# A two-layer trunk: a ring of six adaLN buffers in the first stage, projection weights two tiles ahead, one PE order through the early part, one modulation vector fewer on PE

## The chip, the cores and the metric

The kernel runs on one core of a Trainium2 chip. Its engines have a queue each and run side by side: PE (TensorE, matmuls and transposes), DVE (VectorE), ACT (ScalarE), POOL (GpSimd) and SP (SyncE, which issues most DMAs here). The metric is the device time of one execution in microseconds. Nearly all of the work of the program before the first MLP stands in the first 502 of 2436 us, and the change is made there.

## The reference

x is 256 × 2048, f32, one sequence. Layer 0 mixes tokens with a conformer convolution, layer 1 with differential attention; both are followed by a squared-ReLU MLP of hidden size 8192. The sizes: D = 2048, and each modulation vector needs a 2048 × 2048 matrix (16 MB) against the condition.

```python
cond = jax.nn.silu(c)
for i in range(DEPTH):
    mod = cond @ ada_w[i] + ada_b[i]
    sh_m, sc_m, g_m, sh_f, sc_f, g_f = [m[:, None, :] for m in jnp.split(mod, 6, axis=-1)]
    h = x * (1.0 + sc_m) + sh_m
    y = conformer_conv(h, ...)  # layer 0; layer 1: diff_attention
    x = layer_norm(DEEPNORM_ALPHA * x + g_m * y, ln_mix_g[i], ln_mix_b[i])
    h = x * (1.0 + sc_f) + sh_f
    y = squared_relu_mlp(h, mlp_w1[i], mlp_b1[i], mlp_w2[i], mlp_b2[i])
    x = layer_norm(DEEPNORM_ALPHA * x + g_f * y, ln_ffn_g[i], ln_ffn_b[i])

def conformer_conv(h, w1, b1, w_dw, b_dw, g, b, w2, b2):
    u = h @ w1 + b1                                  # pw1, 2048 x 4096
    a, gt = jnp.split(u, 2, axis=-1)
    u = a * jax.nn.sigmoid(gt)                       # GLU
    u = lax.conv_general_dilated(...) + b_dw         # causal, depthwise, width 31
    u = jax.nn.silu(layer_norm(u, g, b))             # over channels
    return u @ w2 + b2                               # pw2, 2048 x 2048
```

## The kernel before

**Products.** A f32 product is made of three matmuls. ACT rounds a weight half (128 × 1024) to its high part (L462, in later stages L515), DVE, or in places POOL, subtracts to get the low part (L463, L516), and PE multiplies high × high, low × high and high × low (L476 to L478, L551 to L554). The activations are split in the same way (L393, L396). One "half" of a weight tile is twelve such matmuls. A weight tile is 1 MB.

**adaLN vectors.** A vector is summed up in one of two ways, and always from 1 MB tiles that SP loads (L215). A *DVE step* multiplies one tile's two row blocks by the condition and adds them to `aacc` (L243 for the first block, L245 for the others, 128 × 1024 each); at the end PE sums over partitions (`apt`, L228) and DVE adds the bias. A *PE step* multiplies the tile by the condition (`aps`, L286, eight matmuls, spread over column groups), ACT copies the result (`arow`, L290), PE transposes it (`apt`, L269).

**First stage.** pw1 has eight groups of 512 columns. Groups 2, 3 (`ROT`) and 0, 1 (`RES`) are worked first, in five slices of the contraction (`SLICES`: 2, 4, 4, 4 and 2 chunks of 128 rows), since only the slice of the modulated input has to be ready. While slice s is multiplied, the tiles of scale (by DVE) and shift (by PE) for slice s + 1 are used, by `ada_pair` at the halves in `pair_at`; then `end_ada` (PE `apt`, transposes of x, modulation, split by ACT and DVE) makes the next slice's input. `ada_raw` says where an adaLN tile lies: of every four, two are in the `araw` pool and two in halves of `conv_ux`, a buffer that the convolution uses later. Projection weights run four tiles ahead: `load_w` is called four times before the stage and then whenever `split_half` has used up a tile. In the first and last slice a weight tile is half a megabyte (2 chunks of 512 columns).

**T1.** Groups 4 to 7 follow, 32 halves. Between them a written plan (`at(n, ...)`) puts the convolution of the groups that are ready: `glu`, `conv_shift` (copies by ACT and DVE that shift rows), `conv_taps`, `conv_products`, `conv_out`, `conv_tok`, `conv_stats`. `other_vectors` (transposes of four small parameter vectors into columns, L845 to L851) is one item of it, at n = 2. `ADA_T1` DVE steps (20) are spread evenly over the 32 halves, from `dve_q`, which holds the gate G_M and the first half of the scale SC_F.

**Transition.** Between T1 and pw2 stands the last group's chain, `glu(7)`, `conv_shift(7)`, `conv_products`, `conv_out`, `conv_tok`, `conv_stats`, then the channel LayerNorm (L635), then `swish` (PE transposes L1109, ACT silu), three times ahead of pw2. The calls `fill(n)` put n PE steps (SH_F, then the second half of SC_F, from `pe_q`) between these, by `FILL`. Their loads run three ahead, in two `araw` buffers and half of `conv_ux`.

**T2.** pw2 has 32 halves in four groups of 512 columns (`out_proj`). After a half `pump_t2` runs, sixteen times with effect, and spreads what is left of `dve_q` and `pe_q` evenly.

**What sets the order.** `manual_schedule` keeps an engine's instructions in the order in which they are written. Before, the first part (up to and with `conv_shift(7)`) is written so for PE, DVE, ACT and SP together, and a second one for PE alone opens behind it; where none is open, a scheduler sets the order. DVE's is opened again at the start of pw2.

Of the kernel before, what the change touches and what calls it, by code (L numbers as in the profile page):

```python
# [78 lines left out]
def trunk(  # L79
# [371 lines left out]
    def load_raw(src, name):  # L451
        raw = wraw.tile([P, 2048], F32, tag="raw", name=f"w_{name}")[:, :src.shape[1] * NG]
        rv = raw.rearrange("p (a h n) -> p a h n", a=src.shape[1], h=src.shape[2])
        for h in range(src.shape[2]):
            raws["dma"] = nc.sync.dma_start(rv[:, :, h, :], src[:, :, h, :])
        return raw

    def split_raw(rq, name):
# [3 lines left out]
        nc.scalar.copy(hi, rq)  # L462
        nc.vector.tensor_tensor(lo, rq, hi.bitcast(F32), op=ALU.subtract)  # L463
# [381 lines left out]
    def other_vectors():  # L845
        adab.append(as_cols(small_rows["adab1"], "adab1"))
        lnc = as_cols(small_rows["ln"], "ln")
        b1c = as_cols(small_rows["b1"], "b1")
        subg = as_cols(small_rows["subg"], "subg")
        nc.vector.tensor_scalar(subg, subg, 1.0 - LAMBDA_INIT, None, ALU.mult)  # L850
        cv.update(lnc=lnc, b1c=b1c, subg=subg)  # L851
# [726 lines left out]
```

## Time and profile before

| | |
|---|---|
| median of 3 runs | 2439.43 us (2437.01 to 7178.41) |
| profiled execution | 2438.22 us |
| its span, mean granted clock | 2436.4 us, 0.977 |
| first stage | 0 to 196.9 us |
| T1, its start included | 196.9 to 357.8 us |
| transition | 357.8 to 410.9 us |
| T2 | 410.9 to 502.0 us |
| all that follows | 502.0 to 2436.4 us |

The starts are those of the first pw1 matmul after a slice's `end_ada` (slices 2 to 5 start at 70.6, 109.3, 148.0 and 176.8 us), of the last matmul of the first stage, of the end of pw1 and of the first matmul of pw2's bias (L550). Times are microseconds. A row of the stretches gives, for each engine, its busy time in the stretch and the number of instructions; PEclk is the TensorE clock granted there, DMA share is how busy the 16 DMA engines were. A row of waits gives the engine and line that waited, what it waited for, the total, the number of times and the longest. A row of grouped lines gives busy time, mean ns, then idle time ahead of it. MATMUL rows of the timeline are pipelined, so they overlap.

### The profile page before, as it was taken

To read this page: it belongs to the slowest core of one execution; us is meant where nothing else is said; L and a number is where in the kernel's file an instruction comes from. 1 tells how busy PE (TensorE), PEld (TensorE's weight loads), DVE (VectorE), ACT (ScalarE), POOL (GpSimd) and SP (SyncE) were. 2 spreads that over 40 slices of the span, in tenths; PEclk is the share of its full clock that TensorE was granted. 3 is DMA by queue.
4 is the path that set the end of the run, shared out by engine and by line. 5 is a ranking of instruction groups with operands and counts; after the bars stand their busy time and mean duration, and the time that the engine had idled before them with its cause. 6 is when DMAs were issued, how large, how long until landed. Compare 5 with 4: busy or idle time off the path is not lost.

```text
span 2436.4 us, 28627 instructions
## 1 busy us (share of the span) xinstructions
PE 2294.2 (94%) x11223; PEld 1816.7 (75%) x11223; DVE 1744.6 (72%) x1973; ACT 1070.2 (44%) x1376; POOL 243.6 (10%) x162
## 2 busy tenths in 40 slices
PE   3888997989989999999998999998999999999997
PEld 2566763767878888888876888886788888888886
DVE  4666873569798888878868777886867555555566
ACT  2335754344434434434434544443443443443442
POOL 0000000122150000000014200012204000000002
PEclk8999998999999999999999999998999999999999
DMA  9977678857988887888875676685686555555563
GB/s 337 323 245 245 230 260 293 310 202 273 344 294 317 304 308 284 311 314 299 295 255 187 207 238 223 232 289 191 221 287 223 185 186 192 190 188 195 185 224 104
DMA packets 278252, 608.55 MB, mean 250 GB/s; under 512 B 11166, under 2 KB 52708, under 8 KB 264804
## 3 DMA queue, kind: packets, MB, share of 16 engines
q1 hardware_dynamic: 277876, 606.41, 72.1%
q8 instruction: 88, 1.44, 0.2%
q10 hardware_dynamic: 240, 0.30, 0.1%
q14 instruction: 48, 0.39, 0.0%
HBM read 604.54 MB, written 2.13 MB: 249 GB/s over the span
## 4 chain that ended last, share of the span: by engine, by line
PE 81%; DVE 8%; DMA 5%; ACT 2%; issue 2%; SPq 1%; POOL 1%; DVEq 0%; ACTq 0%; POOLq 0%
PE w_ps L551 18%; PE w_ps L553 18%; PE w_ps L554 18%; DMA aw<-in_ada_w_dram 2%; PE cv L755 2%; PE pw_ps L476 2%; PE pw_ps L477 2%; PE pw_ps L478 2%; DMA conv_ux<-in_ada_w_dram 2%; PE aps L286 1%; DVE wl_w L516 1%; PE pw_ps L551 1%; PE qkv_q_ps L554 1%; PE qkv_q_ps L553 1%; PE qkv_q_ps L551 1%
## 5 line engine op out<-in xcount | busy, mean ns | idle before, releaser
L516 DVE TENSOR_TENSOR wl_w<-w_w,wh_w 128x1024 fp32r<-128x1024 f32 x502 | 633.6, 1280 | 333.1 <-ACT wh_w L515 332.7
L515 ACT CAST wh_w<-w_w 128x1024 fp32r<-128x1024 f32 x512 | 537.7, 1053 | 754.2 <-PE w_ps L554 589.1
L551 PE MATMUL w_ps<-wh_w,hm_hi 128*128 128x512 f32 x1024 | 403.8, 394 | 4.8 <-ACT hm_hi L393 4.8
L553 PE MATMUL w_ps<-wl_w,u_hi 128*128 128x512 f32 x1024 | 399.2, 390 | 6.5 <-DVE wl_w L516 6.4
L553 PE MATMUL w_ps<-wl_w,hm_hi 128*128 128x512 f32 x1024 | 400.8, 391 | 4.7 <-DVE wl_w L516 4.6
L554 PE MATMUL w_ps<-wh_w,hm_lo 128*128 128x512 f32 x1024 | 400.9, 392 | 0.9 <-DVE hm_lo L396 0.9
L551 PE MATMUL w_ps<-wh_w,u_hi 128*128 128x512 f32 x1024 | 400.0, 391 | 0.0
L554 PE MATMUL w_ps<-wh_w,u_lo 128*128 128x512 f32 x1024 | 398.6, 389 | 0.0
L312 DVE SCALAR_TENSOR_TENSOR acc<-adaw,cond,acc 128x2048 f32<-128x2048 f32 (+1 forms) x105 | 244.1, 2325 | 0.1
L551 PEld LDWEIGHTS w_ps<-wh_w,hm_hi 128*128 128x128 f32 x1024 | 193.4, 189 | 49.0 <-ACT hm_hi L393 6.5
L553 PEld LDWEIGHTS w_ps<-wl_w,u_hi 128*128 128x128 f32 x1024 | 192.2, 188 | 48.5 <-DVE wl_w L516 9.3
L553 PEld LDWEIGHTS w_ps<-wl_w,hm_hi 128*128 128x128 f32 x1024 | 193.3, 189 | 45.1 <-DVE wl_w L516 5.9
L554 PEld LDWEIGHTS w_ps<-wh_w,hm_lo 128*128 128x128 f32 x1024 | 193.3, 189 | 43.1 <-DVE hm_lo L396 2.5
L551 PEld LDWEIGHTS w_ps<-wh_w,u_hi 128*128 128x128 f32 x1024 | 192.2, 188 | 42.1 <-issue 2.5
L554 PEld LDWEIGHTS w_ps<-wh_w,u_lo 128*128 128x128 f32 x1024 | 192.2, 188 | 40.0
L516 POOL TENSOR_TENSOR wl_w<-w_w,wh_w 128x1024 fp32r<-128x1024 f32 x10 | 24.0, 2405 | 1096.6 <-ACT wh_w L515 1096.6
L476 PE MATMUL pw_ps<-wh_pw,h_hi 128*128 128x512 f32 x256 | 108.9, 425 | 8.6 <-ACT h_hi L393 8.4
L463 DVE TENSOR_TENSOR wl_pw<-w_pw,wh_pw 128x1024 fp32r<-128x1024 f32 x64 | 77.9, 1224 | 46.2 <-ACT wh_pw L462 45.5
L477 PE MATMUL pw_ps<-wl_pw,h_hi 128*128 128x512 f32 x256 | 103.8, 405 | 0.5 <-DVE wl_pw L463 0.5
L478 PE MATMUL pw_ps<-wh_pw,h_lo 128*128 128x512 f32 x256 | 103.3, 403 | 0.0
L245 DVE SCALAR_TENSOR_TENSOR aacc<-aw,cond,aacc 128x1024 f32<-128x1024 f32 (+2 forms) x80 | 81.0, 1012 | 30.8 <-DMA aw<-in_ada_w_dram 29.1
L462 ACT CAST wh_pw<-w_pw 128x1024 fp32r<-128x1024 f32 x64 | 66.2, 1049 | 33.2 <-PE pw_ps L478 13.0
(338 smaller groups left out, 3214.5 us busy)
## 6 DMA issues: line engine op xcount, KB each, us to landing
w_w<-in_mlp_w_dram SPq DMA_DIRECT2D x256, 1024.0 KB, 5.3
adaw<-in_ada_w_dram SPq DMA_DIRECT2D x96, 1024.0 KB, 5.4
aw<-in_ada_w_dram SPq DMA_DIRECT2D x60, 1024.0 KB, 6.8
w_pw<-in_conv_pw_w_dram SPq DMA_DIRECT2D x56, 512.0 KB, 5.3
...
```

What stands on the lines that cost most here:

```text
L245: nc.vector.scalar_tensor_tensor(st["acc"], wv[:, kc % per, :], cond[:, kc:kc + 1], st["acc"], ALU.mult, ALU.add)
L312: nc.vector.scalar_tensor_tensor(st["acc"], w, cond[:, kc:kc + 1], st["acc"], ALU.mult, ALU.add)
L462: nc.scalar.copy(hi, rq)
L463: nc.vector.tensor_tensor(lo, rq, hi.bitcast(F32), op=ALU.subtract)
L476: nc.tensor.matmul(pss[t], lhsT=xh, rhs=wh, start=(kc == first), stop=False)
L477: nc.tensor.matmul(pss[t], lhsT=xh, rhs=wl, start=False, stop=False)
L478: nc.tensor.matmul(pss[t], lhsT=xl, rhs=wh, start=False, stop=(kc == last))
L515: nc.scalar.copy(hi, rq)
L516: eng.tensor_tensor(lo, rq, hi.bitcast(F32), op=ALU.subtract)
L551: nc.tensor.matmul(pss[tt], lhsT=xh, rhs=wh, start=(kc == 0 and job["bias"] is None), stop=False)
L553: nc.tensor.matmul(pss[tt], lhsT=xh, rhs=wl, start=False, stop=False)
L554: nc.tensor.matmul(pss[tt], lhsT=xl, rhs=wh, start=False, stop=(kc == nk - 1))
```

## The change

It has six parts.

1. *Ring of six.* In the first stage `ada_raw` goes round six places: two of `conv_ux`, two in the projection weights' `raw` pool, two of `araw`.
2. *Projection weights two ahead.* Two `load_w` and two more adaLN tiles stand ahead of the stage; in return the slices of two chunks load full 1 MB tiles that hold two groups, so their order becomes 2, 3, 0, 1. At T1's start two more `load_w` bring the weights back to four ahead.
3. *Places in the stage.* `pair_at` and the half at which `end_ada` stands are moved.
4. *Four places for `other_vectors`.* One vector each at n = 2, 3, 6 and 7.
5. *One PE order.* PE's `manual_schedule` opens at the very start and goes through to T2. The load of the silu table is moved ahead of the end of the first part. `conv_shift(7)` has 6 copies on ACT and 10 on DVE in place of 8 and 8.
6. *One vector fewer on PE.* The second half of SC_F goes from `pe_q` (24 steps, now 16) to `dve_q` (24, now 32). `ADA_T1` is 24 in place of 20, and the fills of the transition are 2, 1, 1, 2 (and the one ahead of the gate), with one call fewer.

```diff
-ADA_T1 = 20
-FILL = (3,1,3,2,1)
+ADA_T1 = 24
+FILL = (2, 1, 1, 2)
...
-SHIFT_END = ("act", "dve", "act", "dve")
+END_ACT = (0, 3, 6, 9, 12, 15)
...
             n_raw[0] += 1
-            if n_raw[0] % 4 in (3, 0):
-                return ux[:, n_raw[0] % 4 // 3 * 2048:(n_raw[0] % 4 // 3 + 1) * 2048]
+            n = n_raw[0] % 6
+            if n in (2, 3):
+                return ux[:, (n - 2) * 2048:(n - 1) * 2048]
+            if n in (4, 5):
+                return wraw.tile([P, 2048], F32, tag="raw", name=name)
         return araw.tile([P, 2048], F32, tag="araw", name=name)
...
     add_dve(SC_F, 0, m_scf)
+    add_dve(SC_F, 8, m_scf)
     pe_loads = []
-    for v, m, f00 in ((SH_F, m_shf, 0), (SC_F, m_scf, 8)):
-        for f0 in range(f00, KC, 4):
-            loads, steps = ada_slice_steps(0, v, f0, 4, m, apart=True)
...
+    for f0 in range(0, KC, 4):
+        loads, steps = ada_slice_steps(0, SH_F, f0, 4, m_shf, apart=True)
...
-                if (SHIFT_END if j == 7 else SHIFT)[(r - b) % 4] == "act":
+                if (4 * b + r in END_ACT) if j == 7 else SHIFT[(r - b) % 4] == "act":
...
-    def other_vectors():
-        adab.append(as_cols(small_rows["adab1"], "adab1"))
-        lnc = as_cols(small_rows["ln"], "ln")
...
+    def other_vectors(n):
+        if n == 0:
+            adab.append(as_cols(small_rows["adab1"], "adab1"))
+        elif n == 1:
+            cv.update(lnc=as_cols(small_rows["ln"], "ln"))
...
     engines = mybir.EngineType
-    first_part = tc.manual_schedule(engines={engines.PE, engines.DVE, engines.Activation, engines.SP})
+    early_pe = tc.manual_schedule(engines={engines.PE})
+    early_pe.__enter__()
+    first_part = tc.manual_schedule(engines={engines.DVE, engines.Activation, engines.SP})
...
-    order = [tuple(g for gs in zip(ROT, RES) for g in gs)] * len(SLICES)
+    order = [ROT + RES if nf == 2 else tuple(g for gs in zip(ROT, RES) for g in gs) for f0, nf in SLICES]
     n_first = len(RES + ROT)
-    w_src = [(f"pw1_{g}_{s}", pw1v[:, f0:f0 + nf, :, g * 256:(g + 1) * 256])
-             for s, (f0, nf) in enumerate(SLICES) for g in order[s]]
+    w_src = [(f"pw1_{g}_{s}", pw1v[:, f0:f0 + nf, :, g * 256:(g + 4 // nf) * 256])
+             for s, (f0, nf) in enumerate(SLICES) for g in order[s][::4 // nf]]
...
-    for _ in range(N_RAW):
+    for _ in range(2):
         load_w()
+    for _ in range(2):
+        ada_load.pop(0)()
...
-        pair_at = {4: (0, 1, 2, 3) if n_half == 4 else (0, 2, 4, 5), 2: (2, 5), 0: ()}[nxt]
+        pair_at = {4: (0, 1, 2, 3) if n_half == 4 else (1, 3, 5, 7), 2: (2, 4), 0: ()}[nxt]
...
-                if nxt and h == (3 if n_half == 4 else 6):
+                if nxt and h == (5 if nxt == 2 else n_half - 1):
                     pending()
                     end_ada(s + 1)
...
-            if last and n == 1:
-                pending()
+                if nf == 2:
+                    pending()
+            if last and n == 2:
                 glu(ROT[0])
...
-    at(2, other_vectors)
+    for n in range(4):
+        at((2, 3, 6, 7)[n], other_vectors, n)
...
     for _ in range(2):
+        load_w()
         dve_loads.pop(0)()
...
     glu(7)
     conv_shift(7)
+    warm = small.tile([P, 1], F32, tag="warm", name="warm", bufs=1)
+    nc.scalar.activation(warm, ones[:, 0:1], AF.Silu)
     first_part.__exit__(None, None, None)
-    early_pe = tc.manual_schedule(engines={engines.PE})
-    early_pe.__enter__()
...
     tick(10)
-    fill(FILL[2])
...
-    fill(FILL[3])
+    fill(FILL[2])
...
     for c2 in range(3):
         swish(c2)
-        if c2 < 2:
-            fill(FILL[4])
+    fill(FILL[3])
```

How this moves instructions stands in the order of each queue. First SP's transfers in the first stage, before, from the first adaLN tile of slice 1 (chunk 2) on; `aw` tiles and `conv_ux` are adaLN tiles of 1 MB, `w_pw_2_1` is the projection weight of group 2 and slice 1 (slices are numbered from 0 in names).

```order
L215 DMA aw_1_2_0_205<-in_ada_w_dram 128x4x512
L215 DMA aw_0_2_0_207<-in_ada_w_dram 128x4x512
L215 DMA conv_ux<-in_ada_w_dram 128x4x512 x2
L455 DMA w_pw_2_1_233<-in_conv_pw_w_dram 128x4x256 x2
L455 DMA w_pw_0_1_240<-in_conv_pw_w_dram 128x4x256 x2
L455 DMA w_pw_3_1_269<-in_conv_pw_w_dram 128x4x256 x2
L455 DMA w_pw_1_1_296<-in_conv_pw_w_dram 128x4x256 x2
L215 DMA aw_1_2_2_313<-in_ada_w_dram 128x4x512
L215 DMA aw_0_2_2_315<-in_ada_w_dram 128x4x512
L215 DMA conv_ux<-in_ada_w_dram 128x4x512 x2
```

The same place of SP after:

```order
L218 DMA aw_1_2_0_152<-in_ada_w_dram 128x4x512
L218 DMA aw_0_2_0_154<-in_ada_w_dram 128x4x512
...
L218 DMA aw_1_2_1_205<-in_ada_w_dram 128x4x512
L218 DMA conv_ux<-in_ada_w_dram 128x4x512 x2
L218 DMA aw_0_2_2_227<-in_ada_w_dram 128x4x512
L459 DMA w_pw_2_1_237<-in_conv_pw_w_dram 128x4x256 x2
L218 DMA aw_1_2_3_288<-in_ada_w_dram 128x4x512
L218 DMA aw_0_2_3_290<-in_ada_w_dram 128x4x512
L459 DMA w_pw_0_1_300<-in_conv_pw_w_dram 128x4x256 x2
```

The eight adaLN tiles for the second slice have one projection tile between them instead of four.

Second, PE in the transition, before, from the transposes of the shift vector's first part to the first matmul of pw2; `aps` is an adaLN step, `gb_p` the gate's broadcast, `sw` the swish transposes.

```order
L269 MATMUL apt_3_0_2932<-ident,arow_3_0_2909 128x128 x4
L644 MATMUL gb_p<-ident,mod_2_116 16x128
L286 MATMUL aps_3_4_2925<-conv_ux,condr 32x512 x4
L286 MATMUL aps_3_4_2925<-aw_3_4_2_2911,condr 32x512 x4
L286 MATMUL aps_3_4_2925<-aw_3_4_3_2930,condr 32x512 x4
L286 MATMUL aps_3_8_2981<-conv_ux,condr 32x512 x4
L269 MATMUL apt_3_4_2987<-ident,arow_3_4_2961 128x128 x4
L286 MATMUL aps_3_8_2981<-aw_3_8_1_2955,condr 32x512 x4
L1109 MATMUL sw_3002<-ident,vtok 128x128 x4
L286 MATMUL aps_3_8_2981<-aw_3_8_2_2963,condr 32x512 x4
L1109 MATMUL sw_3018<-ident,vtok 128x128 x4
```

PE at the same place after:

```order
L656 MATMUL gb_p<-ident,mod_2_116 16x128
L272 MATMUL apt_3_0_2951<-ident,arow_3_0_2940 128x128 x4
L289 MATMUL aps_3_4_2974<-aw_3_4_0_2847,condr 32x512 x4
L1127 MATMUL sw_2983<-ident,vtok 128x128 x4
L1127 MATMUL sw_2993<-ident,vtok 128x128 x4
L1127 MATMUL sw_3003<-ident,vtok 128x128 x4
L289 MATMUL aps_3_4_2974<-conv_ux,condr 32x512 x4
L289 MATMUL aps_3_4_2974<-aw_3_4_2_2942,condr 32x512 x4
L289 MATMUL aps_3_4_2974<-aw_3_4_3_2979,condr 32x512 x4
L289 MATMUL aps_3_8_3069<-conv_ux,condr 32x512 x4
L562 MATMUL pw_0_ps_3034<-pw2b_hl,one_2678 128x512 x2
```

One adaLN step stands between the gate's broadcast and the first swish transpose instead of five, and the three swish transposes follow one another. Ahead of this, in the group-7 `glu`, PE's eight transposes (`pa`, `pg`) had two adaLN steps among them before and have none now.

Third, DVE in T2 around the end of pw2's first group, before; `wl_pw` is a subtraction for a half's low part, `aacc` the DVE step, `pw_g` a group's output.

```order
L516 TENSOR_TENSOR wl_pw_1_0_0_3243<-w_pw_1_0_3240,wh_pw_1_0_0_3242 128x1024
L516 TENSOR_TENSOR wl_pw_1_0_1_3259<-w_pw_1_0_3240,wh_pw_1_0_1_3258 128x1024
L245 SCALAR_TENSOR_TENSOR aacc_4_0_2485<-aw_4_0_5_3262,cond,aacc_4_0_2485 128x1024 x2
L697 TENSOR_TENSOR pw_g_3304<-pw_0_ps_3055,conv_ux 128x512
...
L516 TENSOR_TENSOR wl_pw_1_1_1_3322<-w_pw_1_1_3286,wh_pw_1_1_1_3321 128x1024
L516 TENSOR_TENSOR wl_pw_1_2_0_3351<-w_pw_1_2_3348,wh_pw_1_2_0_3350 128x1024
L516 TENSOR_TENSOR wl_pw_1_3_0_3390<-w_pw_1_3_3387,wh_pw_1_3_0_3389 128x1024
```

DVE at the same place after:

```order
L528 TENSOR_TENSOR wl_pw_1_0_0_3229<-w_pw_1_0_3226,wh_pw_1_0_0_3228 128x1024
L528 TENSOR_TENSOR wl_pw_1_0_1_3245<-w_pw_1_0_3226,wh_pw_1_0_1_3244 128x1024
L248 SCALAR_TENSOR_TENSOR aacc_4_8_3048<-aw_4_8_2_3248,cond,aacc_4_8_3048 128x1024 x2
L709 TENSOR_TENSOR pw_g_3282<-pw_0_ps_3034,conv_ux 128x512
...
L528 TENSOR_TENSOR wl_pw_1_1_1_3293<-w_pw_1_1_3264,wh_pw_1_1_1_3292 128x1024
L528 TENSOR_TENSOR wl_pw_1_2_0_3321<-w_pw_1_2_3318,wh_pw_1_2_0_3320 128x1024
L248 SCALAR_TENSOR_TENSOR aacc_4_8_3048<-aw_4_8_3_3340,cond,aacc_4_8_3048 128x1024 x2
```

A DVE step comes after every four halves in T2 in place of after every eight.

More of the change, by code (lines that the diff above doesn't have):

```diff
@@ L348, in trunk @@
     add_dve(SC_F, 0, m_scf)
+    add_dve(SC_F, 8, m_scf)
     pe_loads = []
-    for v, m, f00 in ((SH_F, m_shf, 0), (SC_F, m_scf, 8)):
-        for f0 in range(f00, KC, 4):
-            loads, steps = ada_slice_steps(0, v, f0, 4, m, apart=True)
-            pe_loads.extend(loads)
-            pe_q.extend(steps)
+    for f0 in range(0, KC, 4):
+        loads, steps = ada_slice_steps(0, SH_F, f0, 4, m_shf, apart=True)
+        pe_loads.extend(loads)
+        pe_q.extend(steps)
     m_gf = mod_tile(0, G_F)
@@ L451, in load_raw @@
     def load_raw(src, name):
-        raw = wraw.tile([P, 2048], F32, tag="raw", name=f"w_{name}")[:, :src.shape[1] * NG]
-        rv = raw.rearrange("p (a h n) -> p a h n", a=src.shape[1], h=src.shape[2])
-        for h in range(src.shape[2]):
+        raw = wraw.tile([P, 2048], F32, tag="raw", name=f"w_{name}")
+        rv = raw.rearrange("p (a h n) -> p a h n", a=src.shape[1], h=2)
+        for h in range(2):
             raws["dma"] = nc.sync.dma_start(rv[:, :, h, :], src[:, :, h, :])
-        return raw
+        if src.shape[1] == 4:
+            rw = raw.rearrange("p (q a n) -> p q a n", q=2, a=2)
+        else:
+            rw = raw.rearrange("p (a h q n) -> p q a h n", a=2, h=2, q=2)
+        return [rw[:, q] for q in range(2)]
     def split_raw(rq, name):
@@ L461, in split_raw @@
         lo = wsp.tile([P, 1024], F32R, tag="wlo", name=f"wl_{name}")
-        nc.scalar.copy(hi, rq)
-        nc.vector.tensor_tensor(lo, rq, hi.bitcast(F32), op=ALU.subtract)
         hv = hi.rearrange("p (a n) -> p a n", n=NG)
         lv = lo.rearrange("p (a n) -> p a n", n=NG)
-        return [(hv[:, a, :], lv[:, a, :]) for a in range(1024 // NG)]
+        if len(rq.shape) == 4:
+            hq, lq = [v.rearrange("p a (h n) -> p a h n", h=2) for v in (hv, lv)]
+        else:
+            hq, lq = hv, lv
+        nc.scalar.copy(hq, rq)
+        nc.vector.tensor_tensor(lq, rq, hq.bitcast(F32), op=ALU.subtract)
+        return [(hv[:, a, :], lv[:, a, :]) for a in range(2)]
     def mm_parts(pss, pair, parts, kc0, first, last):
@@ L843, in tap_columns @@
         nc.vector.tensor_reduce(eye, ident.rearrange("p (r c) -> p c r", c=32), axis=AX.X, op=ALU.add)
-    def other_vectors():
-        adab.append(as_cols(small_rows["adab1"], "adab1"))
-        lnc = as_cols(small_rows["ln"], "ln")
[L848 to L851, printed above, removed]
+    def other_vectors(n):
[3 more added lines that the diff above has]
+            cv.update(lnc=as_cols(small_rows["ln"], "ln"))
+        elif n == 2:
+            cv.update(b1c=as_cols(small_rows["b1"], "b1"))
+        else:
+            cv.update(subg=as_cols(small_rows["subg"], "subg"))
+            nc.vector.tensor_scalar(cv["subg"], cv["subg"], 1.0 - LAMBDA_INIT, None, ALU.mult)
     engines = mybir.EngineType
-    first_part = tc.manual_schedule(engines={engines.PE, engines.DVE, engines.Activation, engines.SP})
+    early_pe = tc.manual_schedule(engines={engines.PE})
+    early_pe.__enter__()
+    first_part = tc.manual_schedule(engines={engines.DVE, engines.Activation, engines.SP})
     first_part.__enter__()
@@ L1069, in fill @@
             tick()
-    warm = small.tile([P, 1], F32, tag="warm", name="warm", bufs=1)
-    nc.scalar.activation(warm, ones[:, 0:1], AF.Silu)
     fill(FILL[0])
```

7 lines of the change are left out of this document (3 added, 4 removed).

## The prediction

> **What bounds the kernel now.** I read the page first, to see which engine sets the time.
>
> ```profile
> span 2436.4 us, 28627 instructions
> PE 2294.2 (94%) x11223; PEld 1816.7 (75%) x11223; DVE 1744.6 (72%) x1973; ACT 1070.2 (44%) x1376; POOL 243.6 (10%) x162
> PE 81%; DVE 8%; DMA 5%; ACT 2%; issue 2%; SPq 1%; POOL 1%; DVEq 0%; ACTq 0%; POOLq 0%
> ```
>
> PE is busy for 94% of the span, so a gain is a stretch in which PE stands still now, or PE work that goes away. The change touches only what runs before the first MLP. So the second view is busy time by stretch, with cuts at the starts of slices 2 to 5 of the first stage, the start of T1 (pw1 groups 4 to 7), the transition and T2 (pw2), and with ten microseconds of slice 1 apart.
>
> ```profile
> core 0: us, PE busy (x) PEld busy (x) DVE busy (x) ACT busy (x) POOL busy (x), PEclk, DMA share, GB/s
> 0.00:70.60 70.60, 30.75 (x148) 18.21 (x148) 31.74 (x58) 18.92 (x32) 1.98 (x11) 0.88 1.01 342
> 70.60:109.30 38.70, 31.30 (x148) 21.03 (x149) 25.71 (x37) 10.95 (x14) 0.00 (x0) 0.96 0.97 343
> 109.30:148.00 38.70, 32.31 (x150) 22.15 (x149) 25.99 (x38) 11.89 (x15) 0.00 (x0) 0.91 0.95 319
> 148.00:176.80 28.80, 26.44 (x133) 19.78 (x133) 21.16 (x36) 12.09 (x16) 0.00 (x0) 0.94 0.48 151
> 176.80:196.90 20.10, 19.87 (x96) 16.21 (x96) 11.30 (x16) 13.94 (x21) 0.00 (x0) 1.00 0.78 262
> 196.90:207.30 10.40, 0.95 (x5) 0.47 (x3) 9.28 (x16) 9.34 (x13) 0.00 (x0) 0.68 0.76 268
> 207.30:357.80 150.50, 148.75 (x1356) 107.42 (x1356) 117.91 (x169) 94.63 (x145) 0.00 (x0) 0.99 0.68 231
> 357.80:410.90 53.10, 35.89 (x277) 11.66 (x275) 14.53 (x38) 20.21 (x35) 0.72 (x1) 0.81 0.84 306
> 410.90:502.00 91.10, 91.10 (x443) 64.88 (x440) 55.07 (x58) 34.84 (x42) 12.68 (x5) 1.00 0.89 309
> 50.00:60.00 10.00, 0.37 (x4) 0.20 (x8) 2.99 (x4) 0.00 (x0) 0.00 (x0) 0.50 1.06 377
> ```
>
> Three of these are bound in three ways. In slices 1 to 3 the DMA share is 0.95 or more and PE idles: the transfers set the pace. At T1's start (10.4 us, PE 0.95) PE waits for other engines. In the transition (53.1 us, PE 35.9) much of PE's work is adaLN steps put there as filler. T1's body and T2 are full of PE. Third, who ends PE's waits in the first stage, and the longest of them:
>
> ```profile
> PE aps L286 <- DMA aw<-in_ada_w_dram: 24.4, 4, 14.6
> PE aps L286 <- DMA conv_ux<-in_ada_w_dram: 11.3, 3, 4.4
> PE pw_ps L476 <- ACT h_hi L393: 8.4, 2, 6.8
> 59.63 1.94 PE L286 MATMUL aps<-aw,condr 128*32 128x512 f32 x8 [14.57 <-DMA aw<-in_ada_w_dram]
> ```
>
> PE waits 35.7 us for adaLN tiles, 14.57 of them in one piece for slice 2's tiles. The sum below goes against the profiled execution, 2438.22 us (span 2436.4 and 1.8 around it); the median of the runs shown, 2439.43, is 1.2 above it.
>
> **First stage: ring of six, projection weights two ahead.** The total of buffers is unchanged and so are the bytes; what moves is which transfer is issued first. By the order of SP's transfers, slice 2's last adaLN tile is the 17th megabyte issued instead of the 20th, since two projection tiles less stand ahead and one more is put behind. Three tiles of 1.0486 MB at the 377 GB/s of the 50–60 row are 3 × 2.78 = 8.3 us, out of a wait of 14.57: slice 2 starts about 8 us earlier, for sure within 0 and 8.3.
>
> A full slice moves 12 tiles (8 adaLN, 4 projection), 12.58 MB. At 377 GB/s that is 33.4 us; it takes 38.7. PE is busy 31.3 and 32.3 of it, DVE 25.7 and 26.0, so transfers kept in flight would win at most 5.3 per slice, 10.6 in both. I take 8: `end_ada` now stands behind the last half, its chain of apt, transposes and ACT splits is covered by no matmul, and a projection tile two ahead makes DVE's in-order subtraction wait sooner. Slices 4 and 5 (48.9 us, PE 46.3 busy) have nothing to give. Sum −16; ends 0 and −18.9, and with all 2.4 us that PE idles in slices 4 and 5, −21.3.
>
> The Trainium skill ("DMA: Bandwidth & Descriptors", Specifications) gives about 358 GB/s of HBM per core: by it a slice is 35.1 us and the gain 3.6 in place of 5.3. The trace moved 377 for ten microseconds, so the measured rate decides.
>
> **T1's start.** PE's two waits and DVE's in T1:
>
> ```profile
> PE pt_subg L134 <- DVE cols_adab L136: 5.7, 1, 5.7
> PE pt_b L134 <- DVE conv_ux L806: 3.7, 1, 3.7
> L245 DVE SCALAR_TENSOR_TENSOR aacc<-aw,cond,aacc 128x1024 f32<-128x1024 f32 x37 | 47.4, 1282 | 0.7
> L243 DVE TENSOR_SCALAR aacc<-aw,cond 128x1024 f32<-128x1024 f32 x3 | 2.2, 750 | 4.9 <-DMA aw<-in_ada_w_dram 4.9
> L463 DVE TENSOR_TENSOR wl_pw<-w_pw,wh_pw 128x1024 fp32r<-128x1024 f32 x29 | 35.5, 1225 | 18.2 <-ACT wh_pw L462 17.7
> ```
>
> `other_vectors` asks for four transposes at once, and PE's third half stands behind them: 9.4 us. Split over plan points 2, 3, 6 and 7, only one vector's chain stands there. The tile for which DVE waited 4.9 is now issued ahead of a weight tile. Against this, 24 adaLN steps in 32 halves put the third step ahead of the third half (24·3/32 = 2.25, before 20·3/32 = 1.875), 2 × 1.28 = 2.6 us more on DVE there. The lo split that PE needs waits on DVE anyway, so not all 9.4 goes: −5, ends 0 and −9.4.
>
> **T1's body.** Four more DVE steps of two 1.28 us instructions: 10.3 us. DVE is busy 117.9 of 150.5, so 32.6 us are free, and PE fills 148.75: hidden, 0. Without that cover it is +10.3. The silu table load moves within ACT, which has 55.9 us free here: 0.
>
> **Transition.** The timeline's rows in order of time (start, duration, what ran, in brackets the wait ahead of it), and PE's waits for tiles:
>
> ```profile
> 363.11 1.07 PE L286 MATMUL aps<-aw,condr 128*32 128x512 f32 x8 [2.89 <-DMA aw<-in_ada_w_dram]
> 366.82 5.45 ACT L737 COPY conv_x<-u 32x571 f32<-32x571 f32 x8 [0.58 <-DVE u L806]
> 366.82 3.74 DVE L739 COPY conv_x<-u 32x571 f32<-32x571 f32 x8
> 385.30 2.37 DVE L635 TENSOR_SCALAR vtok<-vtok,cln_mv,cln_rs 128x512 f32<-128x512 f32 x5
> 390.68 1.94 PE L286 MATMUL aps<-aw,condr 128*32 128x512 f32 x8 [2.86 <-DMA aw<-in_ada_w_dram]
> 398.27 0.79 PE L1109 MATMUL sw<-ident,vtok 128*128 128x128 f32 x4
> 410.88 0.71 PE L550 MATMUL pw_ps<-pw2b_hl,one 4*128 4x512 f32 x2
> PE aps L286 <- DMA aw<-in_ada_w_dram: 12.6, 6, 2.9
> ```
>
> Step by step. (1) With one PE order, all eight pa/pg transposes of glu(7) stand ahead of the tile that made PE wait 2.89 and work 1.07 in between: −3.9. (2) `conv_shift(7)` was 8 copies on ACT, 5.45, and 8 on DVE, 3.74; with 6 and 10 it ends with DVE's 10 × 0.467 = 4.7: −0.8. (3) The first swish transpose stood at 398.27, behind five adaLN steps that follow the gate's broadcast (L644), though its input is normalised by 385.3 + 2.4 = 387.7; of these one is left, and I take all but its wait out of the 10.6 us: −10. (4) From the first sw to pw2 it is 12.6 us, four adaLN steps strung between the later sw and their waits; the four now stand in a row behind three sw, 3 × 0.8 + 4 × 1.94 = 10.2 at the slow clock: −2. That is −16.7. A cross-check: 14 tiles stand ahead of pw2 before and 9 after; 53.1/14 = 3.8 a tile, 5 × 3.8 = 19. Between the two I take −18. Ends: −10, if the tiles that are left wait each for its transfer (12.6 in 6 now), and −20.
>
> The Trainium skill ("TensorE: Matmul & The Clock Gate", Part 1) has PE's clock fall to half after an idle window of some 3.4 us, and rise again after as much work, which speaks against taking filler out: by it pw2 would start at half clock, an estimate of +1.7. The trace agrees that this happens: the same eight matmuls take 1.07 at 363 and 1.94 at 390.68, and the clock was 0.50 in the 50–60 row.
>
> **T2.** What is taken from the transition comes back here in part: 8 DVE steps instead of 4, 7 PE steps instead of 10.
>
> ```profile
> DVE aacc L245 <- DMA aw<-in_ada_w_dram: 19.1, 4, 6.0
> DMA to landing us min/median/max: 5.0/6.7/6.8
> ```
>
> PE saves 3 × 1.07 = 3.2 of 91.1. DVE has 55.1 busy and 19.1 waited, 4.8 a step, since each tile is asked for right before its step. Four more steps are 10.3 of work. In the order three of the eight have their tile issued a step earlier, so five wait: 24. Together 55.1 + 10.3 + 24 = 89.4, against PE's 88: no slack is left, and the subtraction that PE's next half needs stands behind each wait. I take 3.2 saved and 8 lost: +5, ends −3 (all hidden) and +13 (10.3 + 24 − 19.1 − 3.2 = 12).
>
> **Sum:** −16 − 5 + 0 − 18 + 5 = −34: 2438.2 − 34 = 2404. After pw2 nothing is changed.
>
> **Rivals.**
> A. All covers hold. The stage gives 21.3, T1's start 9.4, the transition 20, T2 3.2: −54, 2384. For it: the stage is plainly transfer-bound (share 0.95 to 1.01). Against: every chain would have to be free.
> B. The ring isn't six buffers. Two of them are shared with the projection weights and rotate with them, so a projection tile waits until an adaLN tile is consumed, and DVE, which consumes both, waits for the projection tile two ahead: one wait replaces another and the stage gives nothing. Then −5 − 18 + 5 = −18: 2420, with T2 at its worse end 2428. For it: the bytes are the same and DVE waits there as well. Against: slice 2's last tile is issued three megabytes earlier whatever happens.
> C. T2 bound by DVE: +13 there, 2412. For it: the sum of 89.4. Against: POOL takes a few of its subtractions.
> D. Slower: T1 bound by DVE. If each of its 24 steps waited 4.8 as T2's do, 115 us would stand against 22.3 left free: +93, 2497. It makes the kernel slower at all from (22.3 + 34)/24 = 2.3 us a step. Against: 37 instructions of L245 in T1 with 0.7 us idle ahead of them.
>
> **How the numbers follow.** Forecast 0.53 (own range 2392 to 2414), A 0.18, B 0.17, C 0.08, D 0.04. The range takes A's end and B's with T2's worse end, and leaves out D and what lies beyond A: 2384 to 2430. Two per cent, about what a measurement here can tell from no change, is 48.8 us: 2390.6 and 2488.2. A and a sliver of the forecast lie below: faster 0.2. Only D lies above: slower 0.04. Within 0.76.
>
> **What would show it.** Slice 2 starting at about 62 us (was 70.6) and slices 2 and 3 at 35 each confirm the stage; 38 each is B. T1's start: the stretch with PE idle 5 in place of 10. Transition: pw2's first matmul 35 us after T1's last one in place of 53. T2: 96 in place of 91, with waits at the adaLN step on DVE of 24 or more; under 91 it is A, over 100 C. The forecast is wrong if the MLP after it changes, or if T1's body grows by more than 3.

## The result and the profile after

The changed kernel takes 2446.56 us (median of 10 runs), the kernel before 2442.09 in the same sessions: a ratio of 1.0025 with a 95% interval of 1.0014 to 1.0035. It is a quarter of a per cent slower; forecast was 2404. One run of the kernel before took 7178.41 us; no other did, and the median does not show it. The profiled execution took 2448.23 us, its span 2446.4 against 2436.4.

The busy time by stretch for the changed kernel, cut at the same events: starts of slices 2 to 4 (64.41, 103.96, 140.71), the end of the first stage (190.78), the third half of T1 (195.2), the end of T1, the first matmul of pw2 and the starts of pw2's groups. A slice starts with the first product of its own here. In the kernel before, one half of the old slice still stands behind `end_ada` ahead of slices 3 and 4: the starts given for it (109.3 and 148.0) are those behind this half, while the first products after `end_ada` come at 106.45 and 145.20. By the same count its slice 5 starts at 178.2 and not at 176.8; no reading rests on that one.

```profile
33.02:64.41 31.39, 24.04 (x100) 15.12 (x100) 18.03 (x27) 7.94 (x11) 0.00 (x0) 0.81 1.06 375
64.41:103.96 39.55, 33.90 (x150) 24.43 (x150) 25.95 (x37) 11.98 (x15) 0.00 (x0) 0.85 1.06 371
103.96:140.71 36.75, 32.95 (x148) 23.23 (x148) 26.07 (x38) 11.88 (x15) 0.00 (x0) 0.87 0.98 324
190.78:195.20 4.42, 3.70 (x17) 2.81 (x16) 4.28 (x10) 4.33 (x6) 0.00 (x0) 1.00 1.00 394
195.20:359.60 164.40, 151.62 (x1343) 106.58 (x1342) 131.06 (x182) 99.31 (x153) 0.00 (x0) 0.97 0.71 238
359.60:397.41 37.81, 27.83 (x249) 12.58 (x247) 15.41 (x41) 18.22 (x33) 0.72 (x1) 0.82 0.82 296
397.41:438.22 40.81, 34.56 (x145) 25.02 (x141) 17.48 (x18) 15.62 (x23) 5.57 (x2) 0.79 0.70 245
438.22:479.86 41.64, 29.93 (x125) 21.17 (x121) 19.76 (x21) 8.07 (x9) 4.30 (x2) 0.88 0.60 212
479.86:505.79 25.93, 25.93 (x118) 18.61 (x117) 17.07 (x17) 8.42 (x8) 4.33 (x2) 1.00 0.79 279
```

For slice 1 and for pw2 the same view of the kernel before, cut at its own starts and groups:

```profile
31.63:70.63 39.00, 22.80 (x101) 14.05 (x101) 17.95 (x27) 7.75 (x11) 0.00 (x0) 0.78 1.07 373
410.88:440.97 30.09, 30.09 (x157) 21.79 (x153) 17.79 (x17) 16.40 (x24) 4.93 (x2) 1.00 0.86 308
440.97:467.89 26.92, 26.92 (x128) 18.76 (x124) 13.20 (x16) 8.25 (x8) 4.79 (x2) 1.00 0.91 308
467.89:495.31 27.42, 27.42 (x133) 19.27 (x129) 17.52 (x18) 8.99 (x10) 2.97 (x1) 1.00 0.89 310
```

The ledger, in us (before, after, difference, and what was forecast):

| stretch | before | after | difference | forecast |
|---|---|---|---|---|
| start to slice 4 | 148.05 | 140.71 | −7.3 | −16 |
| slices 4 and 5, T1's start | 59.25 | 54.49 | −4.8 | −5 |
| T1's body | 150.5 | 164.4 | +13.9 | 0 |
| transition | 53.1 | 37.8 | −15.3 | −18 |
| pw2, to its fourth group | 84.4 | 108.4 | +24.0 | +5 |
| the rest | 1941.1 | 1940.6 | −0.5 | 0 |

The sum is +10.0, the difference of the spans. Slice 1 (39.0 to 31.4), T1's start (10.4 to 4.4, while slices 4 and 5 took 1.2 more) and the transition gave nearly what was forecast. Slices 2 and 3 gave 1.1 of the 8 (77.4 to 76.3), and T1's body and pw2 took back 38.

One profile stands behind each of these times. Seven of the profiles in this document have the changed kernel's first stage; slice 4 starts in them between 138.3 and 140.7 us, and the stage ends between 186.6 and 190.8. A difference of 2 or 3 us in it is not shown by one pair.

**Slices 2 and 3.** Who waited in the changed kernel, in slice 2 and then in slice 3:

```profile
ACT wh_pw L476 <- DMA w_pw<-in_conv_pw_w_dram: 13.5, 2, 7.3
PE apt L231 <- DVE aacc L248: 4.7, 1, 4.7
```

```profile
ACT wh_pw L476 <- DMA w_pw<-in_conv_pw_w_dram: 11.4, 2, 6.4
PE apt L231 <- DVE aacc L248: 2.6, 1, 2.6
```

PE no longer waits for adaLN tiles; ACT waits for weight tiles, and PE for the scale's last sums at `end_ada`, which no half covers now.

**T1.** PE's waits in T1's body, and what stood in DVE's queue ahead of the longest:

```profile
PE cv L767 <- DVE conv_ux L751: 9.7, 3, 5.1
PE cv L767 <- DVE conv_x L751: 3.1, 2, 1.6
```

```profile
199.36 2.60 DVE L248 SCALAR_TENSOR_TENSOR aacc<-aw,cond,aacc 128x1024 f32<-128x1024 f32 x2
201.88 1.29 DVE L757 TENSOR_TENSOR conv_w<-eye,wct 128x512 f32<-128x512 f32 x2
203.18 0.45 DVE L751 COPY conv_ux<-conv_ux 32x571 f32<-32x571 f32 x1
203.78 6.52 PE L767 MATMUL cv<-conv_ux,conv_w 128*32 128x256 f32 x58 [5.14 <-DVE conv_ux L751]
```

The taps (1.29 us) and the copy (0.45 us) that PE's convolution product needed stood behind an adaLN step of 2.60 us that nobody was waiting for.

**pw2.** Who waited, and the timeline around the longest wait. SPq rows are SP's DMA issues. A row of two lasts from the start of the first to the end of the second; the second one here was issued at 471.92.

```profile
DVE aacc L248 <- DMA aw<-in_ada_w_dram: 46.2, 6, 16.3
PE pw_ps L565 <- DVE wl_pw L528: 18.0, 3, 8.2
```

```profile
463.34 1.06 PE L289 MATMUL aps<-aw,condr 128*32 128x512 f32 x8
464.46 7.82 SPq L218 DMA_DIRECT2D aw<-in_ada_w_dram  x2
469.29 2.60 DVE L248 SCALAR_TENSOR_TENSOR aacc<-aw,cond,aacc 128x1024 f32<-128x1024 f32 x2 [16.30 <-DMA aw<-in_ada_w_dram]
471.81 3.49 DVE L528 TENSOR_TENSOR wl_pw<-w_pw,wh_pw 128x1024 fp32r<-128x1024 f32 x3
473.08 0.80 PE L565 MATMUL pw_ps<-wl_pw,swish_hi 128*128 128x512 f32 x1 [8.24 <-DVE wl_pw L528]
```

DVE stood still for 16.3 us for a tile whose load was issued at 464.46, right after PE had used its own adaLN tile at 463.34: both kinds of tile take turns in two buffers, and PE's are loaded three ahead, so that a DVE tile's load waits for a PE tile that is used several halves later. The subtractions for PE's next halves stood behind it in DVE's queue, and PE waited 8.24 us for them. Of the 24.0 us that pw2 lost, 18.0 are such waits of PE. The other 6.0 are busy time (90.4 us in place of 84.4, for fewer matmul records) at the lower clock of the first two groups.

### The profile page after: what moved, and what is told of

Its sections match the earlier page's. It is cut to its first block, busy times and chain, and to the rows that moved or that the text cites. A ratio compares the mean times of both kernels' runs of the same rounds, so it can differ in the third digit from the quotient of the medians.

```text
span 2446.4 us, 28510 instructions
## 1 busy us (share of the span) xinstructions
PE 2302.1 (94%) x11167; PEld 1829.7 (75%) x11167; DVE 1764.3 (72%) x1988; ACT 1064.3 (44%) x1370; POOL 245.7 (10%) x162
## 4 chain that ended last, share of the span: by engine, by line
PE 70%; issue 18%; DVE 7%; DMA 3%; ACT 1%; POOL 1%; DVEq 0%; ACTq 0%; POOLq 0%; SPq 0%
PE w_ps L563 17%; PE w_ps L566 17%; PE w_ps L565 17%; DVE wl_w L528 1%; PE qkv_q_ps L566 1%; PE qkv_q_ps L565 1%; PE qkv_q_ps L563 1%; PE qkv_v_ps L566 1%; PE qkv_v_ps L563 1%; PE qkv_v_ps L565 1%; DMA w_w<-in_mlp_w_dram 1%; PE qkv_k_ps L566 1%; PE qkv_k_ps L563 1%; PE qkv_k_ps L565 1%; PE pw_ps L563 1%
## 5 line engine op out<-in xcount | busy, mean ns | idle before, releaser
L248 DVE SCALAR_TENSOR_TENSOR aacc<-aw,cond,aacc 128x1024 f32<-128x1024 f32 (+2 forms) x112 | 112.1, 1001 | 48.7 <-DMA aw<-in_ada_w_dram 46.2
L488 PE MATMUL pw_ps<-wh_pw,h_hi 128*128 128x512 f32 x256 | 108.7, 424 | 10.7 <-ACT h_hi L396 10.6
```

The lines of the kernel that those rows point to most:

```text
L248: nc.vector.scalar_tensor_tensor(st["acc"], wv[:, kc % per, :], cond[:, kc:kc + 1], st["acc"], ALU.mult, ALU.add)
L488: nc.tensor.matmul(pss[t], lhsT=xh, rhs=wh, start=(kc == first), stop=False)
```

## The experiments

Below, "slice 4" is the start of its own first product, "T1" goes from the first transpose of the small vectors at the first stage's end to the last product of pw1, "pw2" from its first matmul to its fourth group. All times are us; the kernel before has 148.0, 161.0, 53.0 and 84.4 (slice 4, T1, transition, pw2), the changed kernel 140.7, 169.1, 37.5 and 108.4. A ratio is against the kernel before on the same chip. The kernels with the old places have a half of slice 3 behind `end_ada`; the expectations that put slice 4 at 132 or 128 for them count from the first product after `end_ada`, which comes 2.8 to 3.7 ahead of slice 4's own.

### The vector back on PE

```diff
-ADA_T1 = 24
-FILL = (2, 1, 1, 2)
+ADA_T1 = 20
+FILL = (3, 2, 3, 3)
-    add_dve(SC_F, 8, m_scf)
...
-    for f0 in range(0, KC, 4):
-        loads, steps = ada_slice_steps(0, SH_F, f0, 4, m_shf, apart=True)
+    for v, m, f00 in ((SH_F, m_shf, 0), (SC_F, m_scf, 8)):
+        for f0 in range(f00, KC, 4):
+            loads, steps = ada_slice_steps(0, v, f0, 4, m, apart=True)
```

> The changed kernel with one part undone: the second half of the scale vector SC_F goes back to PE (24 PE steps, ADA_T1 20, four DVE steps in T2), and the fills are 3, 2, 3, 3, so that 14 adaLN tiles stand ahead of pw2 as in the kernel before. Lengths to compare (us, before / changed): T1 from the end of the first stage to its last product 160.9 / 168.8, transition 53.1 / 37.8, pw2 from its first matmul to the start of its fourth group 84.4 / 108.4. Theory, that the vector's move costs both T1 and T2: T1 comes back to about 161, pw2 to about 84, the transition grows to about 49 (14 tiles, but the swish transposes together), total 2446 - 8 - 24 + 11 = about 2425. Rival, that T1's loss comes from the weights two ahead and the four places of the vectors: T1 stays near 168 and the total is about 2433. Rival, that pw2's loss comes from what the ring leaves behind (clock, transfers): pw2 stays above 100.

Measured: 2423.1, ratio 0.992 (0.9905 to 0.9935). T1 155.4, transition 47.8, pw2 84.5. So the sixth part alone turns a kernel that is 0.8% faster into one that is 0.25% slower: it costs 13.7 in T1 and 23.9 in pw2 and wins 10.3 in the transition, five tiles of 2 us. The other 5.2 of the transition's gain (53.0 to 47.8) come with as many tiles as before, from the rest of the change there together: one PE order, the fills' places and the split of the copies. T1 is 5.6 shorter than in the kernel before, about what T1's start won (6.0).

### The first stage as before

The ring, the weights' lead, the tile sizes and the places are put back, the other three parts kept (the lines of the change's diff on `ada_raw`, `load_raw`, `w_src`, `pair_at` and `end_ada`, reversed).

> The changed kernel with the first stage as before (four places for adaLN tiles, weights four ahead, half-megabyte tiles in the slices of two chunks, old places in the slices), all else as changed: four places for the vectors, one PE order, vector moved to DVE. Theory, that the ring is worth 7 us to the start of slice 4 and that T1 loses by its four more DVE steps whatever stands before it: slice 2 starts at 70.6 in place of 64.4, the first stage ends 6 later than in the changed kernel, T1 takes 168 or more, pw2 108: total about 2452. Rival, that T1's loss comes from the weights two ahead: T1 about 161, total about 2445.

Measured: 2459.5, ratio 1.0067 (1.0052 to 1.0082). Slice 2 starts at 71.5, slice 4 at 149.1, the first stage ends 7.2 later than in the changed kernel; T1 171.4, pw2 107.9. T1's and pw2's losses are there without the ring and with weights four ahead, so that rival falls.

### Own places for DVE's tiles in T2

```diff
-            t = ada_raw(f"aw_{i}_{v}_{f0}_{a}", first)
+            name = f"aw_{i}_{v}_{f0}_{a}"
+            t = wraw.tile([P, 2048], F32, tag="raw", name=name) if in_t2[0] else ada_raw(name, first)
...
             while len(q) > max(0, n * (1 - n_t2[0] / ADA_T2)):
+                in_t2[0] = q is dve_q
                 pump_early(q)
+                if in_t2[0] and dve_loads:
+                    dve_loads.pop(0)()
+                in_t2[0] = False
```

> The changed kernel, where DVE's adaLN tiles in T2 lie in the ring of four weight buffers in place of the two buffers that they share with PE's adaLN tiles, and each is loaded one DVE step ahead. Nothing else is changed. Theory, that DVE waits up to 16.3 us because its tile's load waits for a buffer held by a PE tile which PE uses only several halves later: DVE's waits for tiles in T2 fall from 46.2 to under 15, PE's 18 us of waits for the lo part go, pw2 takes 85 to 90 in place of 108.4, total about 2426. Rival, that DVE's added work or the transfer rate is the cause: pw2 stays at 100 or more, total 2440 or more.

Measured: 2421.9, ratio 0.9918 (0.9903 to 0.9932); pw2 85.3. The waits of DVE for tiles in that stretch, and the stretch itself:

```profile
DVE aacc L251 <- DMA aw<-in_ada_w_dram: 0.2, 1, 0.2
396.28:481.57 85.29, 85.29 (x381) 61.96 (x377) 51.48 (x50) 30.95 (x38) 13.36 (x5) 0.94 0.91 337
```

Six of the eight DVE steps stand in these 85.3 us, where the changed kernel has seven in its 108.4: the first one now runs at 352.13, ahead of the transition, and the last one at 492.57, in the fourth group. PE is busy throughout, DVE for 51.5 us (54.3 in the changed kernel), at 337 GB/s where the kernel before moved 308 to 310. So neither the bulk of DVE's work nor the rate is the cause, and 46.2 us of waiting went with the shared buffers. The five profiles with these eight steps and own places have pw2 at 84.0 to 85.3, the five with the shared buffers at 106.9 to 108.4. The transition takes 41.6 in place of 37.5.

The same without the load one step ahead (the two `dve_loads` lines left out):

> As the run with own places for DVE's tiles in T2, but each tile's load stands right at its step, not one step ahead. Theory, that the shared buffers are the cause and the early load only helps: DVE's waits for tiles come to about 5 us a step (about 25 to 40 us in all) with none over 8, pw2 takes 86 to 94. Rival, that the early load is what helps: pw2 stays above 100 with waits of 10 us or more.

Measured: 2425.1, ratio 0.9933 (0.9912 to 0.9954); pw2 84.8, and no wait of DVE for a tile is left in its answer. It is the place that counts. The waits of some 5 us that were expected did not appear.

### 20 steps in T1, 12 in T2

The kernel with own places and `ADA_T1` 20.

> As the kernel with own places for DVE's tiles in T2, and ADA_T1 20 in place of 24: T1 does the 20 DVE steps of the kernel before, T2 does 12 in place of 8. Theory, that T1's loss is the four more DVE steps: T1 comes back from 168.8 to about 161, pw2 has 10.4 us more DVE work (busy 55 + 21 of 90) and stays within 5 of the kernel with own places, total about 2423. Rival, that T1's loss is the order in the first halves or the weights two ahead: T1 stays near 168 and the total is about 2430.

Measured: 2426.0, ratio 0.9943 (0.9924 to 0.9962). T1 153.9 in place of the 165.8 of own places alone: T1's loss is the four steps, and not the order around its start. But pw2 takes 95.2, 10 longer, which the expectation had within 5. ACT waits there 35.2 us for weight tiles in place of 23.3, and DVE 7.3 for adaLN tiles in place of 0.2, at 341 GB/s: four more tiles in T2 are not free. Whether their transfers or their 10.4 us of DVE work cost more is not shown.

### T1's steps behind the convolution

```diff
-            while done < ADA_T1 * n / 32:
-                ...
             mm_parts(pw1[g], hT, w_parts.pop(0), 2 * h, 0, KC - 1)
             tick()
             run_plan(n)
+            while done < ADA_T1 * n / 32:
+                ...
```

> The changed kernel, where in T1 a half's DVE adaLN steps stand behind the half's planned convolution work in DVE's order in place of ahead of it; the same 24 steps. Theory one, that T1 loses because PE's convolution products (it waited 9.7 and 3.1 us there) stand behind DVE steps in DVE's queue, though DVE has time on the whole: T1 falls from 169.1 to about 158, total about 2436. Theory two, that the stretches in which DVE is busy 7.8 of 8 us are short of DVE time itself, so that any place costs the same: T1 stays within 3 of 169, with the wait at the lo part of a weight half in place of the products.

Measured: 2441.9, ratio 1.0002 (0.9989 to 1.0015). T1 158.3 with the same 24 steps. T1 as a stretch of the changed kernel, then of this one, and PE's waits in this one:

```profile
190.78:359.89 169.11, 155.61 (x1361) 109.56 (x1359) 135.59 (x191) 103.65 (x158) 0.00 (x0) 0.97 0.72 242
```

```profile
188.97:347.29 158.32, 151.03 (x1361) 108.25 (x1359) 133.94 (x186) 103.75 (x158) 0.00 (x0) 1.00 0.73 252
PE cv L767 <- DVE conv_ux L751: 5.5, 4, 2.9
PE cv L767 <- DVE conv_x L751: 0.9, 2, 0.7
```

DVE does the same work (133.9 us, 135.6 in the changed kernel) and PE idles 7.3 us in place of 13.5, so over the stage DVE wasn't short of time: the place of the steps in its queue cost 6.2 us of PE's idle time. This repeats. Four profiles with 24 steps ahead of the convolution have 13.5 to 13.6 us of idle time (the old stage and weights three ahead, where T1's first tile comes late, 15.6 and 16.7). Three more with the steps behind it have 7.3, 7.4 and 8.7; with 20 steps it is 4.7 to 5.2 at either place.

The other 4.6 of the 10.8 are the same matmuls at a lower clock (busy 155.6 to 151.0, clock 0.97 to 1.00). The Trainium skill ("TensorE: Matmul & The Clock Gate", Part 1) has PE's clock halved after an idle window of about 3.4 us; the changed kernel has a wait of 5.1 here and this one none above 2.9, which agrees. But the 4.6 are not shown to come from the waits alone: in the run with own places PE has the changed kernel's waits in T1 (9.7, 3.1 and 0.7 us), and it is busy for 152.3 at 0.99. The transition takes 41.5 in place of 37.5, and the total is 4.7 shorter, not 10.8.

### The old places in the slices

```diff
-        pair_at = {4: ... else (1, 3, 5, 7), 2: (2, 4), 0: ()}[nxt]
+        pair_at = {4: ... else (0, 2, 4, 5), 2: (2, 5), 0: ()}[nxt]
-                if nxt and h == (5 if nxt == 2 else n_half - 1):
+                if nxt and h == (3 if n_half == 4 else 6):
```

> The changed kernel with the old places in the slices: tiles used at halves 0, 2, 4, 5, end_ada at half 6 of 8. Ring of six and weights two ahead stay. Changed kernel: slices 2, 3, 4 start at 64.4, 104.0, 140.7. Theory, that the uncovered end_ada chain (5.6 us from apt to the next slice's first product, and 4.7 and 2.6 us of waiting for aacc ahead of it) costs what the ring wins in slices 2 and 3: with one half behind it slice 4 starts 4 to 8 us earlier, at about 134. Rival, that the transfers bound the stage, with the weights two ahead as the wait that is left: the last tiles are needed one half earlier, PE waits for them instead, and slice 4 starts at 140 or later.

Measured: 2442.0, ratio 0.9999 (0.999 to 1.0008). Slice 4 starts at 135.1, 5.6 earlier, and the first stage ends at 182.7, 8.1 earlier. Slices 2 and 3:

```profile
64.23:97.88 33.65, 31.06 (x149) 21.78 (x150) 25.72 (x37) 10.94 (x14) 0.00 (x0) 0.94 1.06 376
97.88:135.07 37.19, 31.70 (x150) 21.80 (x149) 26.03 (x38) 12.72 (x17) 0.00 (x0) 0.95 1.03 344
```

The places' part is smaller on the mean than in this pair: five profiles with the old places start slice 4 at 136.1 and end the stage at 183.7, the seven with the new ones at 139.2 and 188.9, so 3 to 5 us. With a half behind `end_ada` the ring, with the weights two ahead and the larger tiles, gives 14.0 to slice 4's start (135.1 against the 149.1 of the old stage). The Trainium skill ("Perfetto Trace Analysis", Roofline) lets a core that runs alone pull more than its 358 GB/s share; the 376 GB/s over 33.7 us agree.

### Weights three ahead

```diff
-            n = n_raw[0] % 6
+            n = n_raw[0] % 5
...
-            if n in (4, 5):
+            if n == 4:
...
-    for _ in range(2):
+    for _ in range(3):
         load_w()
-    for _ in range(2):
-        ada_load.pop(0)()
+    ada_load.pop(0)()
```

At T1's start one `load_w` in place of two brings the weights back to four ahead.

> The changed kernel with a ring of five adaLN places and projection weights three tiles ahead; all else as changed. Changed kernel: in slices 2 and 3 ACT waited 24.9 us for weight tiles, slice 4 started at 140.7. Theory, that weights two ahead are the wait that took the place of the adaLN tiles: ACT's waits for weights in slices 2 and 3 fall under 10, slice 2 starts about 3 later (its last tile is 18th), slice 4 at about 137. Rival, that the rate of the transfers is the bound whichever tile is late: the wait moves back to adaLN tiles and slice 4 starts within 2 of 140.7 or later.

Measured: 2445.8, ratio 1.0016 (1.0004 to 1.0027). Slice 2 starts at 68.7, slice 4 at 135.6, and ACT no longer waits for a weight tile in slices 2 and 3. So weights two ahead were a wait that took the place of the adaLN tiles' (5.1 us by slice 4 in this pair, 3.6 against the mean of the seven profiles). But T1 takes 174.4 in place of 169.1, and the total is as it was. In T1's start DVE now waits for its first adaLN tile, which it does not in the changed kernel, and PE waits for a subtraction behind it:

```profile
188.66 0.75 DVE L246 TENSOR_SCALAR aacc<-aw,cond 128x1024 f32<-128x1024 f32 x1 [5.29 <-DMA aw<-in_ada_w_dram]
193.47 1.23 DVE L477 TENSOR_TENSOR wl_pw<-w_pw,wh_pw 128x1024 fp32r<-128x1024 f32 x1
194.75 0.80 PE L489 MATMUL pw_ps<-wl_pw,h_hi 128*128 128x512 f32 x1 [6.10 <-DVE wl_pw L477]
```

In all PE idles 3.2 us more in T1 than in the changed kernel. The other 2.1 are slower matmuls, and profiles of the same T1 differ by that much.

### Short fills with the vector on PE

The kernel with the vector back on PE, with `FILL` (2, 1, 1, 2) and own places for T2's DVE tiles.

> The vector back on PE and ADA_T1 20, as in the run of that part alone, but with the changed kernel's short fills 2, 1, 1, 2 (9 adaLN tiles ahead of pw2, 15 PE steps in T2) and own places, one step ahead, for T2's four DVE tiles. That run had T1 155.4, transition 47.8, pw2 84.5, time 2423. Theory, that a tile ahead of pw2 costs 2 us and one in T2 only its 1.07 us of PE time as long as no tile is late: transition 38, pw2 90, total about 2419. Rival, that 15 tiles in T2 through three buffers make PE wait: pw2 97 or more, total 2426 or more.

Measured: 2422.5, ratio 0.9926 (0.9911 to 0.9941). Transition 41.0, pw2 92.7. A tile moved from the transition to pw2 saves 1.4 and costs 1.6 (6.8 and 8.2 over five): to move fillers between these two is worth nothing.

### The remedies together

The edits of old places, of late steps and of own places, in the changed kernel.

> The changed kernel, its moved vector and short fills kept, with the three remedies that were run singly: old places in the slices, T1's DVE steps behind the half's convolution work, own places one step ahead for DVE's tiles in T2. If the three causes add up: slice 4 at 132, T1 158, transition 40, pw2 86; 9.0 + 10.8 + 23 - 4 = 39 less than the changed kernel's 2446, about 2407. If they overlap (a wait goes from one stage to the next): 2415 or more.

Measured: 2420.6, ratio 0.9913 (0.9891 to 0.9935). Slice 4 135.4, T1 160.1, pw2 84.1, nearly as singly; but the transition takes 48.9 in place of 37.5, where late steps and own places alone had 41.5 and 41.6. In their own stretches the remedies won 5.6, 10.8 and 23, in the total 4.6, 4.7 and 24.7; together they come to 26.0, hardly more than own places alone. The transition's first tiles, in the timeline:

```profile
347.30 1.27 DVE L251 SCALAR_TENSOR_TENSOR aacc<-aw,cond,aacc 128x1024 f32<-128x1024 f32 x1
348.60 0.37 SPq L221 DMA_DIRECT2D aw<-in_ada_w_dram  x1
354.28 1.94 PE L292 MATMUL aps<-aw,condr 128*32 128x512 f32 x8 [7.97 <-DMA aw<-in_ada_w_dram]
```

The last DVE step of T1, moved back in DVE's queue, frees its buffer later, and PE's tile is loaded into it at 348.60: the shared pair once more.

With weights three ahead besides:

> The same with a ring of five adaLN places and projection weights three tiles ahead. Alone, that moved slice 4 from 140.7 to 135.6, but T1 took 5 longer. If the weights two ahead still cost once end_ada has a half behind it: slice 4 at 128, total about 2404. If the rate of the transfers is what is left: slice 4 at 132 or later, T1 as long or longer, total 2408 or more.

Measured: 2423.0, ratio 0.9923 (0.9906 to 0.994). Slice 4 at 139.9, T1 161.3, transition 50.7: nothing is won, the rival's reading.

With the vector back on PE and only the remedies of the slices and of T1:

> The kernel with the vector back on PE (2423 us) and the two remedies of the slices and of T1: old places and late steps. Tells whether moving the vector to DVE is worth anything once its costs are gone. Slice 4 at 132 (was 138.3), T1 153 (was 155.4, since it lost little there), transition 48, pw2 84.5: about 2414. If the vector's move is worth the 5 tiles of 2 us in the transition, the kernel with all three remedies is some 7 us faster than this one; if the two are within 3 us, it is worth nothing.

Measured: 2418.7, ratio 0.9905 (0.9888 to 0.9922). Slice 4 136.7, T1 154.3, transition 52.5, pw2 84.8. With 20 steps T1 gains next to nothing from their place: it was 153.6 to 155.4 with the steps ahead of the convolution. Within the intervals the same as with the vector on DVE.

T1's last four DVE tiles in the weight ring too (`in_t2[0] = done + 1 >= ADA_T1 - 4` around the load):

> The kernel with all three remedies, where T1's last four DVE tiles also lie in the ring of weight buffers, so that PE's first tiles of the transition find the pair of adaLN buffers free. Theory, that the pair of shared buffers makes the transition long (first tile 7.97 us late, its load issued behind T1's last DVE step): the transition falls from 48.9 to about 40, total 2420 - 9 = about 2411. Rival, that the transfers are at their rate there, so that an earlier place only moves the wait to a weight tile of T1's end or of pw2: transition 46 or more, or T1 longer by as much, total 2417 or more.

Measured: 2413.3, ratio 0.9878 (0.9863 to 0.9894), the fastest of all. The transition takes 44.4, half of the way to 40; PE's waits for tiles in it fall from 15.7 to 7.0:

```profile
PE aps L292 <- DMA aw<-in_ada_w_dram: 15.7, 4, 8.0
```

```profile
PE aps L292 <- DMA aw<-in_ada_w_dram: 7.0, 2, 5.2
PE pa L811 <- ACT utok L796: 3.9, 1, 3.9
```

The first of these is of the kernel with three remedies, the second of this one.

The same places with the vector on PE and short fills:

> The kernel with the vector back on PE, old places and late steps, here with the short fills 2, 1, 1, 2, own places for T2's DVE tiles and for T1's last four. With the long fills its transition was 52.5, pw2 84.8, time 2418.7. Theory, that a tile ahead of pw2 costs 2 us and the shared pair its wait: transition 40, pw2 91, total about 2413. Rival, that the tiles cost their transfer wherever they stand: transition and pw2 together stay within 3 of 137.3, total 2416 to 2421.

Measured: 2417.5, ratio 0.9897 (0.9879 to 0.9915). Transition 43.5, pw2 92.6, together 136.1 in place of 137.3: the rival's reading.

## Why the prediction was wrong

The forecast of 2404 missed by 43 us, and the sign. By its own terms:

- **First stage, −16: −7.3.** The three-megabytes argument held (slice 2 starts 6.2 earlier, for 8.3). The step that failed is "I take 8" for slices 2 and 3: I named the uncovered `end_ada` chain and took it as a fraction of 10.6, though it comes back in each slice. The run with the old places shows that it, with the later use of the tiles, costs 5.6 by slice 4 and 8.1 by the stage's end in one pair, 3 to 5 on the mean of the profiles. With the old places slice 4 starts 13.0 earlier than in the kernel before, which is close to the 16: it was the third part of the change, and not the ring, that fell short.
- **T1's start, −5: −4.8.** Right, and the start itself gave 6.0. The 5.14 us that the first convolution product waits a few halves later are counted in T1's body.
- **T1's body, 0: +13.9.** This is one of the two large errors. "32.6 us are free: hidden" compares DVE's total with its total; but an instruction delays what stands behind it in DVE's written order, whatever the total is. The vector back on PE takes 13.7 out of T1. The run with the steps behind the convolution keeps the 24 steps and has T1 10.8 us shorter, of which 6.2 are idle time of PE. Rival D had the sign and another mechanism: DVE waited for no tiles in T1.
- **Transition, −18: −15.3.** Right in mechanism; five tiles give 10.3 of it, 2.1 each where 3.8 was the cross-check, and the other parts 5.2 together.
- **T2, +5: +24.** The other large error. The step "five wait: 24" took 4.8 us a wait from the four of before and let it stand for five of the eight. In fact six waits came to 46.2 us by the fourth group and the longest to 16.3, since a load waits for a buffer and not only for its transfer; the rows of before show the transfer's 5 to 6.8 us and hide this. C said +13 and named DVE as the bound; it isn't DVE's work that binds, as the run with own places shows (85.3 us, with DVE busy for 51.5). The estimate of +1.7 for a start of pw2 at half clock stood outside the sum. The start was slow, with 1.22 us for the first two bias products where the kernel before has 0.71, but that is a small part of the 24.

B's sign in the profile was 38 us for slices 2 and 3, and they took 39.6 and 36.8. Its mechanism is there in part: ACT waited 24.9 for weight tiles, and with weights three ahead slice 4 starts 4 to 5 earlier. That the stage gives nothing was wrong.

What isn't settled: why T1's first adaLN tile comes later with weights three ahead, why the same T1 with the same waits takes 165.8 us in two profiles and 169 in two others, why the transition grows by 4 with own places or with late steps alone, and the 4 us that it still keeps over the 40 that were expected of it in the fastest kernel.
